# A hybrid decoder layer: the merge's gate and projection products made token-major, their sum turned for the output projection

## The chip, the core and the metric

The kernel runs on one core of one Trainium2 chip. The metric is the device time of one execution in microseconds. The engines of a core run their own instruction queues and wait for one another by semaphores: TensorE (PE; its weight loads are listed apart as PEld), VectorE (DVE), ScalarE (ACT), GpSimd (POOL), and SyncE (SP), which here only issues transfers from HBM.

## What is computed

One layer over 256 tokens of width 2048. Three branches (a gated linear recurrence "HGRN", causal pooling, a spatial gating unit) each give a 256 x 1024 result. The part that matters here merges them and projects the sum out:

```python
z = x @ w_in[l]
# the last 3 * 2048 columns of z are the gates, gr
gates = jax.nn.sigmoid(gr).reshape(B, S, 3, D)            # D = 2048
merged = (gates[:, :, 0] * (y_hg   @ w_hg_proj[l])        # each y: 256 x 1024
          + gates[:, :, 1] * (y_pool @ w_pool_proj[l])
          + gates[:, :, 2] * (y_sg   @ w_sg_proj[l]))
mix = merged @ w_out[l]
x = layer_norm(DN_ALPHA * x + mix, ln1_g[l], ln1_b[l])
```

A gated feed-forward network of width 5632 and a second layer norm follow.

## The kernel before

**Precision.** Every large product is made of float32 operands that are split in two float32r parts, high and low (`split`, L69: ACT copies the rounded high part, L70; DVE subtracts it from the source, L74). A product is high x high + high x low + low x high. The tile `X` holds the transposed input: for each of 16 blocks k of 128 features (a k-tile) 512 columns, the high parts of the 256 tokens and then their low parts. `y16` holds a branch's result in the same way, in 8 k-tiles.

**Weights.** `pieces` (L79) streams a weight matrix. SP fetches 1 MB pieces into one of two `raw` buffers; each piece is split in two stages of 128 x 1024 elements, into one of four `whi` buffers (ACT) and one of four `wlo` buffers (DVE). So ACT can be at most four stages ahead of PE, and a new piece is fetched when both stages of an older one are split.

**Two forms of a product.** `feat_major` (L114, its inner loop `fm_piece`, L104) makes 256 output features for all 256 tokens, features on the partitions. The weight is stationary, X moves: per k-tile and block of 128 features one matmul of 512 columns (L109, high weight against both parts of X) and one of 256 (L110, low weight against the high part). The low x high result stands in its own columns of the accumulator, so `fm_sum` (L180) adds the two halves afterwards: an ACT copy to `fm_low` and a DVE add. `tok_major` (L137) makes 512 output features with tokens on the partitions. X is stationary, the weight moves: per k-tile and block of 128 tokens three matmuls of 512 columns (L148, L149, L150) that add up in one accumulator. Accumulators are `mm` tiles, three of them; small results go to one of two `ax` tiles.

**The merge.** `merge` (L610) runs once for each branch, in the order pool, gating unit, HGRN. Each run has 8 steps of 256 features: a gate product of 16 k-tiles, `fm_sum` and a sigmoid on ACT; a projection product of 8 k-tiles, `fm_sum`, a multiplication by the gate, and (in the second and third run) an addition to `acc`. In the first two runs the recurrence of one half of the HGRN heads goes on beside it: `hgrn_steps` is a generator, `next(side)` after each product lets it emit its next part, which is DVE and ACT work and a few small PE products. Ahead of each of the first two runs `hgrn` makes six products for its half: four feature-major, a token-major one, two feature-major.

**After the merge.** `acc` is features x tokens, so it is split straight into `mT_t` (which takes the place of X) and used by `tok_major` with `w_out` (L711). Its four column blocks are added to x, and the layer norm follows. The pool `mix`, which holds `acc`, `y16` and the HGRN tiles, is given back before that.

**Order.** PE's order is that of the code. DVE, ACT and SP are ordered by the scheduler by priority; weight splits and the work under `hp()` go first.

Of the kernel before, what the change touches and what calls it, by code (L numbers as in the profile page):

```python
# [8 lines left out]
F32 = mybir.dt.float32  # L9
# [7 lines left out]
P = 128  # L17
S = 256
NT = S // P
# [22 lines left out]
def hybrid_layer(  # L42
# [91 lines left out]
                                         stop=kt == kt_n - 1)  # L134
        return ps

    def tok_major(w2, col, xT, kt_n, big=4, step=2, last=0, home=None, done=None, during={}, ends=(512,)):  # L137
        if last:
            ps = [mm_tile()[:, 0, :] for _ in range(NT)]
        else:  # L140
            both = mm_tile()
            ps = [both[:, t, :] for t in range(NT)]

        def go(kt, t, hi, lo, k, o=None, w=slice(0, 512), first=0):
            o = ps[t] if o is None else o
            xs = slice(t * P, (t + 1) * P)
            xl = slice(S + t * P, S + (t + 1) * P)
            nc.tensor.matmul(o[:, w], lhsT=xT(kt)[:, xs], rhs=hi[:, k, w], start=kt == first, stop=False)  # L148
            nc.tensor.matmul(o[:, w], lhsT=xT(kt)[:, xs], rhs=lo[:, k, w], start=False, stop=False)  # L149
            nc.tensor.matmul(o[:, w], lhsT=xT(kt)[:, xl], rhs=hi[:, k, w], start=False, stop=kt == kt_n - 1)  # L150

        kept = []
        for k0, n, hi, lo in pieces(w2, col, 512, kt_n, big, step, home=home):
            if k0 < kt_n - last:
                for k in range(n):
                    for t in range(NT):
                        go(k0 + k, t, hi, lo, k)
            else:
                kept.append((k0, n, hi, lo))
                for k in range(n):  # L160
                    go(k0 + k, 0, hi, lo, k)
        if last:
            done(0, ps[0], 0, 512)
        c0 = 0
        for c1 in ends if last else ():
            left = last
            o = mm_tile()[:, 0, :] if c0 else ps[1]
            for k0, n, hi, lo in kept:
                for k in range(n):
                    go(k0 + k, 1, hi, lo, k, o, slice(c0, c1), kept[0][0] if c0 else 0)  # L170
                    left -= 1
                    for f in during.get(left, ()):
                        f()
            done(1, o, c0, c1)
            c0 = c1
        return ps
# [27 lines left out]
    one_c, eps_c, mhalf_c, zero_c = (cc[:, i:i + 1] for i in range(4))  # L204

    def rstd_of(pool, st, want_nmr=True):
        mv = pool.tile([P, 4], F32, name="ln_mv", bufs=2)
        nc.vector.bn_aggr(out=mv[:, 0:2], in_=st)
        nc.vector.tensor_scalar(out=mv[:, 1:2], in0=mv[:, 1:2], scalar1=LN_EPS, scalar2=None, op0=ALU.add)
        nc.gpsimd.tensor_tensor(out=mv[:, 1:2], in0=mv[:, 1:2], in1=mhalf_c, op=ALU.pow)  # L210
        if want_nmr:
            nc.vector.tensor_scalar(out=mv[:, 2:3], in0=mv[:, 0:1], scalar1=-1.0, scalar2=None, op0=ALU.mult)
            nc.gpsimd.tensor_tensor(out=mv[:, 2:3], in0=mv[:, 2:3], in1=mv[:, 1:2], op=ALU.mult)  # L213
        return mv[:, 0:1], mv[:, 1:2], mv[:, 2:3]
# [24 lines left out]
    def fm_a():  # L239
        return mix.tile([P, 2, S], F32, name="fm_a", bufs=2)  # L240
# [364 lines left out]
            stt(o[:, hs], o[:, hs], normg[:, h0 + h:h0 + h + 1], og[:, hs], ALU.mult, ALU.mult)  # L605
        res.append(bc(o, S))

    acc = mix.tile([P, KD, S], F32, name="acc")

    def merge(first, gi, y, wp, side=()):  # L610
        side = iter(side)
        gcol = 7168 + D * gi
        for j in range(8):
            ps = feat_major(win, gcol + 256 * j, xT, KD)
            gt = fm_a()
            fm_sum(gt, ps, mix)
            with hp():
                act(gt, gt, AF.Sigmoid)
            next(side, None)
            ps = feat_major(wp, 256 * j, lambda k: y[:, k, :], KW)  # L620
            aj = acc[:, 2 * j:2 * j + 2, :]
            pr = fm_b()
            fm_sum(pr, ps, mix)
            with hp():
                if first:
                    mul(aj, pr, gt)
                else:
                    mul(pr, pr, gt)
                    add(aj, aj, pr)
            next(side, None)  # L630
        for _ in side:
            pass

    o_hg = []
    merge(True, 1, y_pool, w_pool_proj[0], hgrn_steps(0, *hgrn(0), o_hg))
# [1 line left out]
    split(y_hg[:, 0:4, 0:S], y_hg[:, 0:4, S:2 * S], o_hg[0])  # L637
    merge(False, 2, y_sg, w_sg_proj[0], hgrn_steps(1, *hgrn(1), o_hg))
    split(y_hg[:, 4:8, 0:S], y_hg[:, 4:8, S:2 * S], o_hg[1])
    merge(False, 0, y_hg, w_hg_proj[0])  # L640
    mT_t = x_tile()
    for j in range(8):
        split(mT_t[:, 2 * j:2 * j + 2, 0:S], mT_t[:, 2 * j:2 * j + 2, S:2 * S], acc[:, 2 * j:2 * j + 2, :])
    mix_cm.__exit__(None, None, None)

    def mT(k):
        return mT_t[:, k, :]

    ff_cm = tc.tile_pool(name="ff", bufs=1, reuse_waits="tile")
    ff = ff_cm.__enter__()  # L650
# [57 lines left out]

    for j in range(3):
        cs = slice(512 * j, 512 * (j + 1))  # L710
        ps = tok_major(wout, 512 * j, mT, KD)  # L711
        with hp():
            for t in range(NT):
                stt(x1[:, t, cs], x1[:, t, cs], ALPHA, ps[t], ALU.mult, ALU.add)
                nc.vector.bn_stats(out=st1[:, t, j, :], in_=x1[:, t, cs])
# [206 lines left out]
```

## Time and profile before

| what | us |
|---|---|
| median of 3 runs (1602.33, 1602.33, 1611.42) | 1602.33 |
| the profiled execution | 1603.08 |
| its span, first to last instruction | 1601.4 |
| PE busy | 1582.5 |
| DVE busy | 1030.9 |
| ACT busy | 868.3 |
| merge runs, by the span's clock | 245.6 to 392.2, 481.0 to 627.6, 627.6 to 763.0 |

The profile takes one execution apart. Each instruction has a line of the kernel, an engine, the tiles that it writes and reads, a start and a duration. Matmuls are pipelined: a matmul's own duration is longer than the distance to the next one's start, so for PE the distance between starts is what counts, and a stretch with known numbers of matmuls gives it. "PEclk" is the granted TensorE clock as a share of the full 2.4 GHz. In the tile names buffer numbers are left out: `t` is `t4`, `y` is `y16`.

### The profile page before, as it was taken

What the parts mean: (1) busy time and instruction counts of PE and PEld (TensorE: products, weight loads), DVE (VectorE), ACT (ScalarE), POOL (GpSimd) and SP (SyncE); (2) the same over time, 40 slices, a digit from 0 to 9 for tenths busy, and PEclk for the clock granted to TensorE, in tenths of its full rate; (3) what the DMA queues carried; (4) which work ended last, traced back from release to release, by engine and by line L of the source; (5) the groups of instructions that cost most, each with busy time, mean ns of one, the idle gap of its engine ahead of it and who ended that gap; (6) DMA issues with size and microseconds to landing.
All of it is one profiled execution on the core that took longest, in us unless ns stands there. A gap on an engine that the chain in (4) does not pass through costs nothing. (4 is left out here: it accounts for less than half of the span.)

```text
span 1601.4 us, 21561 instructions
## 1 busy us (share of the span) xinstructions
PE 1582.5 (99%) x8673; PEld 1369.0 (85%) x8673; DVE 1030.9 (64%) x1244; ACT 868.3 (54%) x1022; POOL 48.6 (3%) x116
## 2 busy tenths in 40 slices
PE   9999999999999999999998999999999999999997
PEld 7888888888888888888888888888888888888886
DVE  6666547876448866665657766676666766455446
ACT  5555558766458756544435555555555555433332
POOL 1100000000000000000004000000000000000001
PEclk9999999999999999999999999999999999999998
DMA  7656565554555556655763555555565556655553
GB/s 252 230 185 196 184 202 167 183 184 158 184 186 182 177 170 206 210 185 184 244 206 129 184 188 195 196 185 184 190 197 192 184 186 235 210 185 198 196 186 130
DMA packets 254084, 305.20 MB, mean 191 GB/s; under 512 B 5148, under 2 KB 211540, under 8 KB 253472
## 3 DMA queue, kind: packets, MB, share of 16 engines
q1 hardware_dynamic: 251776, 294.67, 56.1%
q0 software_dynamic: 2208, 9.16, 1.6%
q8 instruction: 68, 1.11, 0.3%
q14 instruction: 32, 0.26, 0.1%
HBM read 301.71 MB, written 2.10 MB: 190 GB/s over the span
## 5 line engine op out<-in xcount | busy, mean ns | idle before, releaser
L74 DVE TENSOR_TENSOR wlo<-raw,whi 128x1024 fp32r<-128x1024 f32 x541 | 659.9, 1222 | 502.4 <-ACT whi L70 500.8
L70 ACT ACTIVATE whi<-raw 128x1024 fp32r<-128x1024 f32 x543 | 571.5, 1056 | 647.6 <-PE mm L109 366.2
L109 PE MATMUL mm<-X,whi 128*128 128x512 f32 x1408 | 495.5, 397 | 0.5 <-DVE X L74 0.4
L109 PE MATMUL mm<-x1T,whi 128*128 128x512 f32 x1376 | 477.1, 394 | 0.0
L110 PE MATMUL mm<-X,wlo 128*128 128x256 f32 x1408 | 394.0, 280 | 0.0
L110 PE MATMUL mm<-x1T,wlo 128*128 128x256 f32 x1376 | 381.9, 278 | 0.0
L109 PEld LDWEIGHTS mm<-X,whi 128*128 128x128 f32 x1408 | 265.0, 188 | 62.7 <-PE mm L270 0.6
L109 PEld LDWEIGHTS mm<-x1T,whi 128*128 128x128 f32 x1376 | 258.8, 188 | 59.4
L110 PEld LDWEIGHTS mm<-X,wlo 128*128 128x128 f32 x1408 | 265.7, 189 | 0.2
L110 PEld LDWEIGHTS mm<-x1T,wlo 128*128 128x128 f32 x1376 | 258.2, 188 | 0.0
L109 PE MATMUL mm<-y,whi 128*128 128x512 f32 x384 | 137.2, 397 | 0.0
L148 PE MATMUL mm<-whi,aT 128*128 128x512 f32 (+1 forms) x352 | 135.5, 385 | 0.0
L150 PE MATMUL mm<-whi,aT 128*128 128x512 f32 (+1 forms) x352 | 135.4, 385 | 0.0
L149 PE MATMUL mm<-wlo,aT 128*128 128x512 f32 (+1 forms) x352 | 135.4, 385 | 0.0
L110 PE MATMUL mm<-y,wlo 128*128 128x256 f32 x384 | 108.4, 282 | 0.0
L148 PE MATMUL mm<-whi,X 128*128 128x512 f32 x228 | 88.9, 390 | 0.0
L150 PE MATMUL mm<-whi,X 128*128 128x512 f32 x228 | 88.9, 390 | 0.0
L149 PE MATMUL mm<-wlo,X 128*128 128x512 f32 x228 | 88.8, 390 | 0.0
L109 PEld LDWEIGHTS mm<-y,whi 128*128 128x128 f32 x384 | 72.4, 188 | 16.8
L150 PEld LDWEIGHTS mm<-whi,aT 128*128 128x128 f32 x352 | 66.2, 188 | 13.1
L149 PEld LDWEIGHTS mm<-wlo,aT 128*128 128x128 f32 x352 | 66.2, 188 | 13.1
L148 PEld LDWEIGHTS mm<-whi,aT 128*128 128x128 f32 x352 | 66.2, 188 | 12.9
(180 smaller groups left out, 1221.1 us busy)
## 6 DMA issues: line engine op xcount, KB each, us to landing
raw<-in_w_in_dram SPq DMA_DIRECT2D x102, 1024.0 KB, 5.0
raw<-in_w_up_dram SPq DMA_DIRECT2D x88, 1024.0 KB, 5.1
raw<-in_w_down_dram SPq DMA_DIRECT2D x44, 1024.0 KB, 5.0
raw<-in_w_out_dram SPq DMA_DIRECT2D x16, 1024.0 KB, 5.1
raw<-in_w_pool_proj_dram SPq DMA_DIRECT2D x8, 1024.0 KB, 5.3
raw<-in_w_sg_proj_dram SPq DMA_DIRECT2D x8, 1024.0 KB, 5.3
raw<-in_w_hg_proj_dram SPq DMA_DIRECT2D x8, 1024.0 KB, 5.3
x<-in_x_dram POOLq DMA_DIRECT2D x4, 512.0 KB, 9.1
```

Of the source, the lines that this page charges most:

```text
L70: nc.scalar.activation(out=o, in_=a, func=f, **kw)
L74: low.tensor_tensor(out=lo, in0=src, in1=hi.bitcast(F32), op=ALU.subtract)
L109: nc.tensor.matmul(ps[:, c, :], lhsT=hi[:, k, cs], rhs=xT(kt)[:, 0:512], start=kt == 0, stop=False)
L110: nc.tensor.matmul(ps[:, c, 0:256], lhsT=lo[:, k, cs], rhs=xT(kt)[:, 0:256], start=False, stop=kt == kt_n - 1)
L148: nc.tensor.matmul(o[:, w], lhsT=xT(kt)[:, xs], rhs=hi[:, k, w], start=kt == first, stop=False)
L149: nc.tensor.matmul(o[:, w], lhsT=xT(kt)[:, xs], rhs=lo[:, k, w], start=False, stop=False)
L150: nc.tensor.matmul(o[:, w], lhsT=xT(kt)[:, xl], rhs=hi[:, k, w], start=False, stop=kt == kt_n - 1)
```

## The change

The merge's gate and projection products are made by `tok_major` in blocks of 512 features, four blocks to a run instead of eight steps of 256. `acc` becomes tokens x features. The sigmoid reads the accumulator directly, the product with the gate too; `fm_sum` is not called in the merge. The generator's parts are now emitted after the gate product's k-tiles 4 and 10 (the new argument `mid` of `tok_major`), after the gate product, and after the projection product. The third run is written apart, as `last_merge`: first the four gate products, kept in a tile that takes the place of `y_sg`, then the four projection products. As `acc` now has tokens on the partitions, TensorE turns it: `turn(j)` transposes eight 128 x 128 blocks into two `ax` tiles and splits them into `mT_t`, in the middle of the next projection product, and for the last block in the middle of the first output product, which is now issued ahead of giving back `mix`. The tile `ln_mv` grows from 4 to 16 floats, by which tiles allocated behind it move by 64 bytes (in `mix`: `lv`, `masks`, `y16`, `fm_a`, `fm_b`, `sc`; later the kept output weights and all tiles of the feed-forward stage).

```diff
--- before.py
+++ after.py
@@ -134,7 +134,7 @@
                                          stop=kt == kt_n - 1)
         return ps
 
-    def tok_major(w2, col, xT, kt_n, big=4, step=2, last=0, home=None, done=None, during={}, ends=(512,)):
+    def tok_major(w2, col, xT, kt_n, big=4, step=2, last=0, home=None, done=None, during={}, ends=(512,), mid={}):
         if last:
             ps = [mm_tile()[:, 0, :] for _ in range(NT)]
         else:
@@ -155,6 +155,8 @@
                 for k in range(n):
                     for t in range(NT):
                         go(k0 + k, t, hi, lo, k)
+                    for f in mid.get(k0 + k, ()):
+                        f()
             else:
                 kept.append((k0, n, hi, lo))
                 for k in range(n):
@@ -204,7 +206,7 @@
     one_c, eps_c, mhalf_c, zero_c = (cc[:, i:i + 1] for i in range(4))
 
     def rstd_of(pool, st, want_nmr=True):
-        mv = pool.tile([P, 4], F32, name="ln_mv", bufs=2)
+        mv = pool.tile([P, 16], F32, name="ln_mv", bufs=2)
         nc.vector.bn_aggr(out=mv[:, 0:2], in_=st)
         nc.vector.tensor_scalar(out=mv[:, 1:2], in0=mv[:, 1:2], scalar1=LN_EPS, scalar2=None, op0=ALU.add)
         nc.gpsimd.tensor_tensor(out=mv[:, 1:2], in0=mv[:, 1:2], in1=mhalf_c, op=ALU.pow)
@@ -605,31 +607,66 @@
             stt(o[:, hs], o[:, hs], normg[:, h0 + h:h0 + h + 1], og[:, hs], ALU.mult, ALU.mult)
         res.append(bc(o, S))
 
-    acc = mix.tile([P, KD, S], F32, name="acc")
-
-    def merge(first, gi, y, wp, side=()):
+    acc = mix.tile([P, NT, D], F32, name="acc")
+
+    def columns(j):
+        return slice(512 * j, 512 * (j + 1))
+
+    def open_gate(gi, j, home, mid={}):
+        ps = tok_major(win, 7168 + D * gi + 512 * j, xT, KD, mid=mid)
+        with hp():
+            for t in range(NT):
+                act(home[t], ps[t], AF.Sigmoid)
+
+    def pass_gate(first, j, y, wp, home, mid={}):
+        ps = tok_major(wp, 512 * j, lambda k: y[:, k, :], KW, mid=mid)
+        with hp():
+            for t in range(NT):
+                at = acc[:, t, columns(j)]
+                if first:
+                    mul(at, ps[t], home[t])
+                else:
+                    mul(home[t], ps[t], home[t])
+                    add(at, at, home[t])
+
+    def gates():
+        return [fm_a().rearrange("p c s -> p (c s)") for _ in range(NT)]
+
+    def merge(first, gi, y, wp, side):
         side = iter(side)
-        gcol = 7168 + D * gi
-        for j in range(8):
-            ps = feat_major(win, gcol + 256 * j, xT, KD)
-            gt = fm_a()
-            fm_sum(gt, ps, mix)
-            with hp():
-                act(gt, gt, AF.Sigmoid)
+
+        def step():
             next(side, None)
-            ps = feat_major(wp, 256 * j, lambda k: y[:, k, :], KW)
-            aj = acc[:, 2 * j:2 * j + 2, :]
-            pr = fm_b()
-            fm_sum(pr, ps, mix)
-            with hp():
-                if first:
-                    mul(aj, pr, gt)
-                else:
-                    mul(pr, pr, gt)
-                    add(aj, aj, pr)
-            next(side, None)
+
+        for j in range(4):
+            home = gates()
+            open_gate(gi, j, home, {4: [step], 10: [step]})
+            step()
+            pass_gate(first, j, y, wp, home)
+            step()
         for _ in side:
             pass
+
+    def last_merge(gi, y, wp):
+        kept = mix.tile([P, 8, 512], F32, name="y16", bufs=2)
+        homes = [[kept[:, 2 * j + t, :] for t in range(NT)] for j in range(4)]
+        for j in range(4):
+            open_gate(gi, j, homes[j])
+        mT_t = x_tile()
+
+        def turn(j):
+            for t in range(NT):
+                with hp():
+                    tp = bc(ax_tile(), P)
+                    for i in range(4):
+                        k = 4 * j + i
+                        nc.tensor.transpose(tp[:, i, :], acc[:, t, k * P:(k + 1) * P], ident)
+                    to = mT_t[:, 4 * j:4 * j + 4, :]
+                    split(to[:, :, t * P:(t + 1) * P], to[:, :, S + t * P:S + (t + 1) * P], tp)
+
+        for j in range(4):
+            pass_gate(False, j, y, wp, homes[j], {KW - 3: [lambda j=j: turn(j - 1)]} if j else {})
+        return mT_t, {6: [lambda: turn(3)]}
 
     o_hg = []
     merge(True, 1, y_pool, w_pool_proj[0], hgrn_steps(0, *hgrn(0), o_hg))
@@ -637,14 +674,13 @@
     split(y_hg[:, 0:4, 0:S], y_hg[:, 0:4, S:2 * S], o_hg[0])
     merge(False, 2, y_sg, w_sg_proj[0], hgrn_steps(1, *hgrn(1), o_hg))
     split(y_hg[:, 4:8, 0:S], y_hg[:, 4:8, S:2 * S], o_hg[1])
-    merge(False, 0, y_hg, w_hg_proj[0])
-    mT_t = x_tile()
-    for j in range(8):
-        split(mT_t[:, 2 * j:2 * j + 2, 0:S], mT_t[:, 2 * j:2 * j + 2, S:2 * S], acc[:, 2 * j:2 * j + 2, :])
-    mix_cm.__exit__(None, None, None)
+    mT_t, turn_last = last_merge(0, y_hg, w_hg_proj[0])
 
     def mT(k):
         return mT_t[:, k, :]
+
+    first_out = tok_major(wout, 0, mT, KD, mid=turn_last)
+    mix_cm.__exit__(None, None, None)
 
     ff_cm = tc.tile_pool(name="ff", bufs=1, reuse_waits="tile")
     ff = ff_cm.__enter__()
@@ -708,7 +744,7 @@
 
     for j in range(3):
         cs = slice(512 * j, 512 * (j + 1))
-        ps = tok_major(wout, 512 * j, mT, KD)
+        ps = tok_major(wout, 512 * j, mT, KD) if j else first_out
         with hp():
             for t in range(NT):
                 stt(x1[:, t, cs], x1[:, t, cs], ALPHA, ps[t], ALU.mult, ALU.add)
```

On DVE, in the first run's beginning, before the change: the rows from the addition that prepares the recurrence's decay. `wlo` rows are weight stages, here those of the second gate product and the first of the second projection; `t4`, `seg` and `lv` rows are the recurrence.

```order
L61 TENSOR_TENSOR t4_2225<-t4_2225,t4_1456 128x1024
L74 TENSOR_TENSOR wlo_2402<-raw_2399,whi_2401 128x1024
L481 SCALAR_TENSOR_TENSOR t4_2241<-seg_78,t4_2225 128x256 x3
L74 TENSOR_TENSOR wlo_2422<-raw_2399,whi_2421 128x1024
L481 SCALAR_TENSOR_TENSOR t4_2241<-seg_78,t4_2225 128x256
L58 TENSOR_TENSOR t4_2225<-t4_2241,t4_2224 128x4x128 x2
L58 TENSOR_TENSOR lv_2446<-t4_2241 128x512
L74 TENSOR_TENSOR wlo_2458<-raw_2455,whi_2457 128x1024
L64 TENSOR_TENSOR t4_2224<-t4_2224,t4_1457 128x1024
L74 TENSOR_TENSOR wlo_2478<-raw_2455,whi_2477 128x1024
L61 TENSOR_TENSOR fm_a_2393<-mm_2308,fm_low_2394 128x512
L74 TENSOR_TENSOR t4_2251<-t4_2224,t4_2250 128x1024
```

The same place after the change, from the same addition on; `wlo_2315`, `wlo_2331` and `wlo_2349` are the first three of the four stages of the first projection product.

```order
L61 TENSOR_TENSOR t4_2184<-t4_2184,t4_1456 128x1024
L74 TENSOR_TENSOR wlo_2315<-raw_2312,whi_2314 128x1024
L483 SCALAR_TENSOR_TENSOR t4_2200<-seg_78,t4_2184 128x256 x4
L58 TENSOR_TENSOR t4_2184<-t4_2200,t4_2183 128x4x128 x2
L74 TENSOR_TENSOR wlo_2331<-raw_2312,whi_2330 128x1024
L58 TENSOR_TENSOR lv_2382<-t4_2200 128x512
L64 TENSOR_TENSOR t4_2183<-t4_2183,t4_1457 128x1024
L74 TENSOR_TENSOR wlo_2349<-raw_2346,whi_2348 128x1024
L64 TENSOR_TENSOR lv_2382<-lv_2382,t4_1457 128x512
L74 TENSOR_TENSOR t4_2210<-t4_2183,t4_2209 128x1024
L58 TENSOR_TENSOR lv_2386<-t4_2200,t4_2184 128x4x64 x2
L58 TENSOR_TENSOR lv_2447<-t4_2200 128x512
```

The same recurrence work moved up: one more pair of subtractions follows, and then the fourth stage, so that all of it stands among four weight stages, where before it was spread over about eight.

On PE, in the last projection products after the change: the transposes of the first block (two groups of four, into the two `ax` tiles) stand between the sixth and the seventh k-tile of the second projection product (`mm_5552`).

```order
L149 MATMUL mm_5552<-wlo_5590,y16_3182 128x512
L150 MATMUL mm_5552<-whi_5589,y16_3182 128x512
L663 MATMUL ax_5605<-id2_69,acc_1455 128x128 x4
L663 MATMUL ax_5612<-id2_69,acc_1455 128x128 x4
L148 MATMUL mm_5552<-whi_5619,y16_3182 128x512
L149 MATMUL mm_5552<-wlo_5620,y16_3182 128x512
```

Before the change the last projection product runs into the first output product with nothing between them.

```order
L109 MATMUL mm_6496<-y16_3438,whi_6519 128x512
L110 MATMUL mm_6496<-y16_3438,wlo_6520 128x256
L148 MATMUL mm_6580<-whi_6583,X_6545 128x512
L149 MATMUL mm_6580<-wlo_6584,X_6545 128x512
L150 MATMUL mm_6580<-whi_6583,X_6545 128x512
```

Four such groups of eight transposes are new on PE, and the pairs of 512 and 256 columns have given way to triples of 512.

## Rows read from the trace of the kernel before

**Rows 1.** The page, busy time of each engine, with share and instructions.

```profile
PE 1582.5 (99%) x8673; PEld 1369.0 (85%) x8673; DVE 1030.9 (64%) x1244; ACT 868.3 (54%) x1022; POOL 48.6 (3%) x116
```

**Rows 2.** Waits of PE: waiting line, releaser, total us, times, longest.

```profile
PE ax L700 <- issue: 1.9, 1, 1.9
...
PE mm L109 <- DVE X L74: 0.4, 1, 0.4
```

**Rows 3.** Waits of ACT, its two costliest: releaser, us in total, times, longest.

```profile
ACT whi L70 <- PE mm L109: 366.2, 283, 2.6
ACT whi L70 <- PE mm L150: 169.3, 107, 4.3
```

**Rows 4.** PE by stretches: window, length, busy (matmuls touching it), clock, DMA, GB/s.

```profile
627.60:763.00 135.40, 135.40 (x770) 1.00 0.63 204
763.00:831.00 68.00, 68.00 (x302) 1.00 0.64 224
245.60:392.20 146.60, 146.60 (x868) 1.00 0.55 176
481.00:627.60 146.60, 146.60 (x868) 1.00 0.54 173
263.00:274.10 11.10, 11.10 (x65) 1.00 0.55 178
644.40:655.70 11.30, 11.30 (x66) 1.00 0.72 224
392.20:436.60 44.40, 44.40 (x258) 1.00 0.57 187
458.40:481.00 22.60, 22.60 (x129) 1.00 0.54 170
```

**Rows 5.** PE's timeline at the layer norm's transposes: start, us, engine, line, operation.

```profile
848.02 0.66 PE L700 MATMUL ax<-id,x 128*128 128x128 f32 x4 [1.17 <-POOL x L695]
848.44 0.47 PE L148 MATMUL mm<-khi,X 128*128 128x512 f32 x1
...
849.67 0.40 PE L150 MATMUL mm<-khi,X 128*128 128x512 f32 x1
849.91 0.60 PE L700 MATMUL ax<-id,x 128*128 128x128 f32 x4
850.26 0.48 PE L148 MATMUL mm<-khi,X 128*128 128x512 f32 x1
```

**Rows 6.** PE's timeline at another group of eight transposes.

```profile
57.51 1.03 PE L361 MATMUL ax<-id,t 128*128 128x128 f32 x8
58.30 0.48 PE L148 MATMUL mm<-whi,X 128*128 128x512 f32 x1
```

**Rows 7.** The layer norm's transposes as instructions on the tile ax: duration ns min/median/max.

```profile
L700 PE MATMUL ax<-id,x x32: 272/273/329, 848.0 to 867.7; 128*128 128x128 f32 x32
```

**Rows 8.** ACT and DVE groups of the third run: count, busy us, mean ns, idle.

```profile
L70 ACT ACTIVATE whi<-raw 128x1024 fp32r<-128x1024 f32 x48 | 50.4, 1059 | 69.9 <-PE mm L109 53.3 <-DMA raw<-in_w_in_dram 7.9 <-DMA raw<-in_w_hg_proj_dram 7.7
L70 ACT ACTIVATE fm_low<-mm 128x512 f32<-128x512 f32 x16 | 9.3, 578 | 0.0
...
L74 DVE TENSOR_TENSOR wlo<-raw,whi 128x1024 fp32r<-128x1024 f32 x49 | 59.6, 1224 | 55.5 <-ACT whi L70 55.5
...
L61 DVE TENSOR_TENSOR fm_b<-mm,fm_low 128x512 f32<-128x512 f32 x8 | 5.5, 684 | 0.0
```

**Rows 9.** DVE's instructions on the tile t4 in one stretch: length, busy (count).

```profile
267.40:286.40 19.00, 10.74 (x16) 1.00 0.53 168
```

**Rows 10.** DMA issues of the merge's weights: count, KB each, median us to landing.

```profile
raw<-in_w_in_dram SPq DMA_DIRECT2D x102, 1024.0 KB, 5.0
raw<-in_w_pool_proj_dram SPq DMA_DIRECT2D x8, 1024.0 KB, 5.3
```

## The prediction

> **What bounds the kernel now.** I read the page's busy times first. PE is busy for 1582.5 of 1601.4 us, DVE and ACT for about two thirds and a half [rows 1]. A busy PE is not yet a bound, so the next view is the list of PE's waits. The longest in the whole span is 1.9 us, at the first layer norm, and the only one that falls on a product beside it is 0.4 us at the start [rows 2]. In the merge PE waits for nothing. The view from the other side agrees: ACT, which makes the high parts of the weights, stands 366.2 and 169.3 us waiting for PE to give back a weight buffer [rows 3]. So the weights are ahead, the engines that feed PE have room, and in the merge time is PE's own: number of matmuls by the distance from one to the next.
>
> That distance comes from stretches with known counts. The third run of the merge has 8 x (64 + 32) = 768 matmuls of the feature-major form in 135.4 us (the view counts 770, two only touch the stretch): 176.3 ns each, half of them 512 and half 256 columns wide [rows 4]. Right behind it 300 token-major matmuls of 512 columns, three full output products and two k-tiles, take 68.0 us: 226.7 ns each [rows 4]. The granted clock is 1.00, the 2.4 GHz level, in both. A k-tile for 512 features needs eight of the first kind, 1.410 us, or six of the second, 1.360 us. The columns are as many (3072). What differs is that each matmul costs a little beyond its columns, and there are two fewer.
>
> **The change part by part.** *Products.* The third run's 768 matmuls become 576: 576 x 0.2267 = 130.6 us for 135.4, a gain of 4.8. The first two runs have the same 768, with 98 or 100 small ones between. Some of their gate products run at 11.1 us where those of the third need 11.3 [rows 4], so I take 4.6 each. Together -14.0 (bound -14.4, if they equal the third).
>
> *Interruptions.* The small products of the recurrence stay, in eleven groups to a run, but now stand in token-major streams. Rows show what a group does there: after four transposes the six matmuls of a k-tile run from 848.44 to 849.91, 1.47 us where six at 226.7 need 1.36 [rows 5]. That is 0.11 us lost to each restart. The removed form's figures had their restarts in them, so I add 11 x 0.11 x 2 = +2.4. Bounds: 0, if a restart costs as in the old form, and +3.
>
> *Transposes.* Four groups of eight are new on PE. Eight like them take 0.79 us (57.51 to 58.30) [rows 6], four 0.42 or 0.35 [rows 5]. With a restart a group of eight is 0.9: +3.7 in all, between 3.1 without restarts and 3.8. Their own durations are 0.27 us [rows 7], but the next starts 0.1 us later. The Trainium skill, page "TensorE: Matmul & The Clock Gate", Part 4, gives about 275 ns for a transpose within a kernel; the duration in the trace agrees, the spacing doesn't, and by that figure per transpose 32 would cost an estimated 8.8 us and most of the gain would be gone.
>
> *State of the stream.* Feature-major products run at two rates: the 256 matmuls of the second half's first four products take 44.4 us (173.4 each), and the 128 that follow a token-major product 22.6 (176.6) [rows 4]. After the change those 256 follow a token-major product too: 256 x 3.2 ns = +0.8. Bounds 0 and 0.8.
>
> *ACT and DVE.* The calls of `fm_sum` go: 48 copies of 0.578 us and 48 additions of 0.684 [rows 8], 27.7 us of ACT and 32.8 of DVE. They had cover, PE never waited for them, so this gives nothing back. Sigmoids, gate multiplications, additions to `acc` and splits into `mT_t` keep number and size. The splits now read what PE turned. The last ones follow the seventh k-tile of the first output product and are needed by its k-tile 12, five k-tiles or 6.8 us later; four operations of 0.6 to 0.7 us fit. The turn of a block stands six k-tiles, 8.2 us, behind the end of the product that made it, and four DVE operations of 0.7 us need to be done by then. In `last_merge` the four gate products need `y_sg`'s tile, whose last reader is PE just before; the first write is a sigmoid 21.8 us later. The weights stay 1 MB a piece, in the same number.
>
> *The grown tile.* The 64-byte moves change no shape or count. I cost them at nothing; if the rate of the down projection, 1056 matmuls, moved by the 3.2 ns above, it would be 3.4 us.
>
> *The weights' lead.* This is where cover could end. With four buffers a stage can be split once PE has done the one four before it, so it is ready 3 x 2.72 us, less 1.06 and 1.22 for its two halves [rows 8], ahead: 5.9 us. At the start of the first two runs the recurrence's preparation stands on DVE among four weight stages, as the order shows: 16 instructions, 10.7 us [rows 9]. With four stages of 1.22 that is 15.6 us, in which PE does four stages and one small group, 11.3 us. The lead falls by 4.3 to about 1.6 us, at the projection's last stage. I take no stall, and up to one late landing of 5.3 us [rows 10] to a run as a bound.
>
> *Sum.* -14.0 + 2.4 + 3.7 + 0.8 = -7.1 us. The profiled execution has 1601.4 of span and 1603.08 in all, 0.05% over the median, so the span should fall to 1594.3 and the median from 1602.33 to **1595.2**.
>
> **The rivals.**
> *The weights run late (slower).* Place: the first projection product of the first two runs, where the lead is thin. If ACT's exponentials, which stand in one queue with the weight copies and wait for DVE's results, add more than 1.6 us to DVE's stretch, PE waits. A stage split late also gives its `raw` buffer back late, so that the next fetch, 5.3 us, shows. It decides from 3.6 us of stall to a run on, where the gain is gone. At one exposed landing to each run: 1595.2 + 10.6 = 1605.8. For it: the crowding just counted. Against it: about 536 us of ACT waiting for PE's buffers, so the lead recovers everywhere else [rows 3].
>
> *Nothing is gained by the form.* If a matmul's time went by its columns alone, 512 of them would be two thirds of a pair of the old form, 2/3 x 2 x 176.3 = 235 ns, six of these 1.410 us, and the products would cost what they did. Then the additions remain: 1602.33 + 2.4 + 3.7 + 0.8 = 1609.2. Against it stand the 300 matmuls at 226.7 with the same stationary X and the same moving weights [rows 4]. The Trainium skill, page "TensorE: Matmul & The Clock Gate", section Back-to-back issue gap, is near this rival: columns over 2.4 GHz and 2.5 ns. By that a k-tile would be an estimated 1.300 us in the old form and 1.295 in the new, 1.5 us over the 288 k-tiles, and the change a loss. The trace's spacing for 512 columns is 226.7 ns rather than 215.8, so here it is too small.
>
> *More is gained.* Restarts cost no more than in the old form, the stream keeps its faster rate, and the transposes cost 3.1: -14.4 + 3.1 = -11.3, which is 1591.0. Against it the 0.11 us of the restart row.
>
> **How the numbers follow.** About 1% (16 us) is what a measurement of this kernel can tell from no change. The forecast, a gain of 5 to 9 us, has 0.60; more gain 0.14; late weights 0.16; no gain by the form 0.05; the rest, an effect of the moved tiles or a stall in the transposes, 0.05. The range from 1590.5 to 1604 takes in the forecast, the greater gain and the milder half of the late weights, with some 0.83. A gain of over 1% would need 16 us, more than all the product gain: 0.03. A loss of over 1% needs waits in most of the blocks of all runs: 0.05. Within 1%: 0.92.
>
> **What the profile after would show.** Products: the stretch of the third run to the first output product has 576 matmuls of token-major form at about 227 ns between starts; 230 or more would break the largest term. Restarts: the k-tile behind a group of small products takes about 1.47 us. Transposes: 0.8 us between the start of the first of eight and the next product. Late weights: waits of PE on DVE's `wlo` near the first projection products, about 25 us into the first and second run; with none over half a microsecond that rival falls. ACT's table loads and DVE's busy time should fall with no trace of it in the span. I am wrong if PE's waits rise by over 3 us, or if feed-forward or down projection change their length.

## The result and the profile after

The changed kernel takes 1616.03 us (median of 20 executions) against 1602.67 for the kernel before: 1.0053 times as long [1.0036, 1.0069]. The forecast was 1595.2, between 1590.5 and 1604. So it lies within the 1% that can hardly be told from no change, but on the other side of it, and outside the range. Nineteen executions stand in two groups, 7 at 1606.7 to 1609.2 us and 12 at 1615.1 to 1619.6 (one more, of 2440.73 us at a granted clock of 0.60, is left aside). The two groups turn out to be part of the answer. The profiled execution, 1615.63 us with a span of 1613.9, is one of the upper group.

The page after, first the busy times. Against [rows 1] DVE and ACT are relieved by 28 and 39 us. The removed calls of `fm_sum` make 32.8 us of DVE's work and 27.7 of ACT's [rows 8], and ACT's table loads fell as well, from 46 to 34 (59.0 us to 43.6). PE is busy 13 us longer with 544 instructions fewer.

```profile
PE 1595.4 (99%) x8129; PEld 1349.1 (84%) x8129; DVE 1002.7 (62%) x1196; ACT 829.0 (51%) x962; POOL 47.9 (3%) x116
```

The span cut at PE's stages tells where the time went. Columns: window, length, then busy time and count of PE, PEld, DVE, ACT and POOL, granted clock, DMA share, GB/s. First before: merge, output products with the layer norm, up products of the feed-forward network, down projection (a tail of 28 us behind it is as long in both).

```profile
245.60:763.00 517.40, 517.40 (x2982) 453.20 (x2981) 345.13 (x410) 324.99 (x381) 4.03 (x6) 1.00 0.57 184
763.00:873.30 110.30, 106.09 (x546) 89.98 (x545) 73.66 (x83) 48.55 (x55) 17.60 (x14) 1.00 0.54 186
873.30:1350.40 477.10, 477.10 (x2755) 417.63 (x2754) 329.55 (x430) 271.42 (x345) 5.44 (x44) 1.00 0.59 193
1350.40:1573.40 223.00, 223.00 (x986) 184.83 (x985) 111.54 (x102) 89.76 (x87) 0.00 (x0) 1.00 0.59 201
```

The same four stages after.

```profile
245.30:758.00 512.70, 512.18 (x2431) 427.46 (x2430) 317.00 (x364) 286.41 (x322) 4.04 (x6) 1.00 0.57 190
758.00:870.20 112.20, 108.66 (x553) 91.91 (x552) 72.56 (x81) 47.62 (x52) 17.22 (x14) 0.98 0.48 161
870.20:1356.40 486.20, 486.20 (x2754) 421.69 (x2754) 330.38 (x430) 271.56 (x345) 5.45 (x44) 1.00 0.58 189
1356.40:1586.00 229.60, 229.60 (x986) 185.04 (x985) 111.83 (x102) 89.79 (x87) 0.00 (x0) 1.00 0.57 196
```

The merge gained 4.7 us. The two largest losses are in stages whose code and instructions did not change: +9.1 in the up products (2752 matmuls, 173.4 ns each before and 176.7 after) and +6.6 in the down projection (984 matmuls, 226.7 and 233.3). PE waits in neither, and the clock is 1.00 in both. Output products and layer norm lose 1.9, of which 0.9 is the last group of transposes that now stands there. The other 1.0 goes with the clock, 0.98 in that stage: behind PE's wait of 2.0 us at the layer norm it stands near 0.5, the 1.2 GHz level, and six matmuls of 512 columns start 0.43 us apart, where 0.23 is usual.

```profile
849.50:852.00 2.50, 2.50 (x9) 0.53 0.95 304
```

In the profile of before the clock stays at 1.00 behind the same wait (1.9 us [rows 2]). It fell there in all six profiles with the new merge and in three of the seven with the old one, so whether the change has a part in it is not shown.

PE's waits after (waiting line, releaser, us in total, times, longest) have one new entry, half a microsecond for a low weight part; the others are those of [rows 2] and the start.

```profile
PE ax L736 <- issue: 2.0, 1, 2.0
...
PE mm L149 <- DVE wlo L74: 0.5, 1, 0.5
```

And ACT waits for PE's weight buffers as long as before: 287.8 and 285.5 us for 366.2 and 169.3 [rows 3]. The weights are ahead, so the time is still PE's own.

```profile
ACT whi L70 <- PE mm L150: 287.8, 182, 3.0
ACT whi L70 <- PE mm L109: 285.5, 222, 1.8
```

Inside the merge the new form has two rates. PE by stretches: 238 gate matmuls of the third run, on X, and 84 projection matmuls behind them, on `y16`.

```profile
655.00:709.00 54.00, 54.00 (x240) 1.00 0.58 194
710.80:730.30 19.50, 19.50 (x86) 1.00 0.55 191
```

That is 226.9 ns for the first, as forecast, but 232 for the second (232.4 by the starts, 710.77 to 730.29 us). PE's timeline at a group of transposes in the projection (start, us, operation) shows the forecast 0.79 us [rows 6], then a restart: the second matmul behind it starts 0.31 us after the first.

```profile
730.29 1.03 PE L663 MATMUL ax<-id,acc 128*128 128x128 f32 x8
731.08 0.48 PE L148 MATMUL mm<-whi,y 128*128 128x512 f32 x1
731.39 0.39 PE L149 MATMUL mm<-wlo,y 128*128 128x512 f32 x1
```

So three things need a cause: the rate of token-major products on `y16` and in the down projection, the rate of the up products, and the new wait.

### The profile page after: what moved, and what is told of

Read it like the earlier page. It is cut to its first block, busy times and chain, and to the rows that moved or that the text cites. A ratio compares the mean times of both kernels' runs of the same rounds, so it can differ in the third digit from the quotient of the medians.

```text
span 1613.9 us, 20294 instructions
## 1 busy us (share of the span) xinstructions
PE 1595.4 (99%) x8129; PEld 1349.1 (84%) x8129; DVE 1002.7 (62%) x1196; ACT 829.0 (51%) x962; POOL 47.9 (3%) x116
## 5 line engine op out<-in xcount | busy, mean ns | idle before, releaser
L70 ACT ACTIVATE whi<-raw 128x1024 fp32r<-128x1024 f32 x543 | 571.3, 1056 | 689.7 <-PE mm L150 287.8
L109 PE MATMUL mm<-x1T,whi 128*128 128x512 f32 x1376 | 486.3, 399 | 0.0
L110 PE MATMUL mm<-x1T,wlo 128*128 128x256 f32 x1376 | 386.5, 281 | 0.0
L148 PE MATMUL mm<-whi,X 128*128 128x512 f32 x612 | 239.5, 391 | 0.0
L149 PE MATMUL mm<-wlo,X 128*128 128x512 f32 x612 | 238.3, 389 | 0.5 <-DVE wlo L74 0.5
L150 PE MATMUL mm<-whi,X 128*128 128x512 f32 x612 | 238.3, 389 | 0.0
L109 PE MATMUL mm<-X,whi 128*128 128x512 f32 x640 | 225.3, 397 | 0.5 <-DVE X L74 0.4
L110 PE MATMUL mm<-X,wlo 128*128 128x256 f32 x640 | 179.1, 280 | 0.0
L109 PEld LDWEIGHTS mm<-X,whi 128*128 128x128 f32 x640 | 120.1, 188 | 29.2 <-DVE X L74 0.6
L149 PEld LDWEIGHTS mm<-wlo,X 128*128 128x128 f32 x612 | 114.9, 188 | 24.2 <-DVE wlo L74 1.1
L150 PEld LDWEIGHTS mm<-whi,X 128*128 128x128 f32 x612 | 114.9, 188 | 24.0
L148 PEld LDWEIGHTS mm<-whi,X 128*128 128x128 f32 x612 | 114.9, 188 | 23.5
L110 PEld LDWEIGHTS mm<-X,wlo 128*128 128x128 f32 x640 | 120.7, 189 | 0.1
```

Of the source, the lines that this page charges most:

```text
L70: nc.scalar.activation(out=o, in_=a, func=f, **kw)
L109: nc.tensor.matmul(ps[:, c, :], lhsT=hi[:, k, cs], rhs=xT(kt)[:, 0:512], start=kt == 0, stop=False)
L110: nc.tensor.matmul(ps[:, c, 0:256], lhsT=lo[:, k, cs], rhs=xT(kt)[:, 0:256], start=False, stop=kt == kt_n - 1)
```

## The experiments

**The token-major rate.** `aT`, the tile that the down projection holds stationary, is one of those that the growth of `ln_mv` moved by 64 bytes. My theory was that the place of the tile sets the distance between matmuls. The rival: something else in the changed program, such as the merge's new order or the layer norm's different timing. Two runs part them: the change without the growth, and the growth without the change.

```diff
--- the changed kernel
+++ e1_after_mv4
-        mv = pool.tile([P, 16], F32, name="ln_mv", bufs=2)
+        mv = pool.tile([P, 4], F32, name="ln_mv", bufs=2)
```

> The changed kernel with ln_mv at 4 floats again, so that y16 and aT lie where they lay before the change. Theory A (the address of the stationary tile sets the distance of token-major matmuls): the down projection's 984 first matmuls go back from 233.3 to 226.7 ns, so 6.5 us come back: about 1600.3 us, or 1609.5 in an execution whose feed-forward products run at their slower rate (486 us instead of 477). Theory B (the rates are states that a stream falls into by what ran before it, addresses do nothing): the down projection stays at 233.3 and the time stays at 1606.8 or 1616.

```diff
--- the kernel before
+++ e2_before_mv16
-        mv = pool.tile([P, 4], F32, name="ln_mv", bufs=2)
+        mv = pool.tile([P, 16], F32, name="ln_mv", bufs=2)
```

> The kernel before with ln_mv at 16 floats, nothing else: y16 and aT move by 64 bytes. Theory A (address): the down projection goes from 226.7 to 233.3 ns a matmul, 1602.5 + 6.5 = 1609 us, and if the feed-forward stage's slower rate comes with the move as well, mostly 1618. Theory B (state, by what ran before): 1602.5, as the kernel before.

PE by stretches, the down projection without the growth:

```profile
1349.00:1572.00 223.00, 223.00 (x985) 1.00 0.58 201
```

and the kernel before with the growth alone, its up products and its down projection:

```profile
876.40:1353.50 477.10, 477.10 (x2755) 1.00 0.58 193
1353.50:1583.10 229.60, 229.60 (x987) 1.00 0.57 195
```

The 6.6 us follow the growth, in both directions. As medians, the first takes 1603.12 us (1.0010 [0.9988, 1.0031]), in two groups again, 7 of 12 executions at 1600.9 to 1603.7 and 5 at 1610.7 to 1612.7. Its lower group is 5 us below that of the changed kernel, not 6.6: with `y16` at its old place the first 84 projection matmuls take 19.6 us (233.4 ns), and late weights cost some 2 us in the last run's gate products.

```profile
712.90:732.50 19.60, 19.60 (x86) 1.00 0.55 191
```

The second takes 1615.1 (1.0077 [1.0050, 1.0104]), again in two groups (1611.6 to 1615.1 and 1621.3 to 1621.9). That is some 3 us more than the down projection explains. In its profile the layer norm's stage has 1.1 of them, by the lower clock told of above, and the merge 2.0: its feature-major products run at a slower rate more often, the first run for example in 147.1 us where [rows 4] have 146.6.

```profile
245.60:392.70 147.10, 147.10 (x867) 1.00 0.54 175
```

The up products kept their rate in this profile, so the growth is not what sets it.

In e3 `ln_mv` grows in the pool `mix` alone, and there far enough that `y16` stands as `X` does, 384 bytes behind a multiple of 512. `aT` stays where it was before.

```diff
--- the changed kernel
+++ e3_y_as_X
-        mv = pool.tile([P, 16], F32, name="ln_mv", bufs=2)
+        mv = pool.tile([P, 32 if pool is mix else 4], F32, name="ln_mv", bufs=2)
```

> The changed kernel with ln_mv at 32 floats in the mix pool and 4 in the ff pool: aT lies as before the change, y16 at the same offset within 512 bytes as X (384). Theory A: projection products run at 226.8 instead of 232 to 234 ns, down projection at 226.7: 1606.8 - 6.5 - 3.5 = 1596.8 us where the feed-forward products run at their faster rate. Theory B: 1606.8 or 1616 as the changed kernel.

PE by stretches: the first gate product and the other three of the last run, its first 84 projection matmuls, and the down projection.

```profile
621.30:710.30 89.00, 87.71 (x385) 1.00 0.58 203
710.30:729.40 19.10, 19.10 (x86) 1.00 0.55 199
1355.30:1578.40 223.10, 223.10 (x986) 1.00 0.59 201
```

The projection has come down to 227 ns and the down projection is back. The median, 1607.02 us (0.9998 [0.9977, 1.0020]), tells little: 5 executions at 1598.1 to 1602.7, 7 at 1606.8 to 1609.6. The gate products, whose 384 matmuls should take 87.1, still take 89.0.

The map: the 22 tiles of `aT` in groups of three, each 64 bytes further than the last, in the kernel before. One execution then has several rates, if it is the place, and one if it isn't.

```diff
--- the kernel before
+++ e4_map
-    aT_t = [up.tile([P, 2, 2 * S], F32R, name=f"aT{j}", bufs=1) for j in range(KF // 2)]
+    aT_t = []
+    for j in range(KF // 2):
+        raw = up.tile([P, 4 * S + (16 if j % 3 == 2 else 0)], F32R, name=f"aT{'abcdefgh'[j // 3]}{j}", bufs=1)
+        aT_t.append(raw[:, 0:4 * S].rearrange("p (k s) -> p k s", s=2 * S))
```

> The kernel before with the 22 aT tiles in eight groups, named aTa to aTh, each group 64 bytes further on within 512 than the one before: offsets 128, 192, 256, 320, 384, 448, 0, 64. Theory A: the distance of the down projection's matmuls changes from group to group, aTa 226.7 and aTb 233.3 ns, the others show which offsets are slow. Theory B: one distance over all groups, or changes that do not follow the groups in all four column blocks.

PE's timeline, the last matmul of each group of 36 in one column block: the steps between them are 8.18, 8.40, 8.36, 8.25 and 8.19 us.

```profile
1410.36 0.39 PE L150 MATMUL mm<-whi,aTh 128*128 128x512 f32 x1
...
1418.54 0.39 PE L150 MATMUL mm<-whi,aTa 128*128 128x512 f32 x1
...
1426.94 0.39 PE L150 MATMUL mm<-whi,aTb 128*128 128x512 f32 x1
...
1435.30 0.40 PE L150 MATMUL mm<-whi,aTc 128*128 128x512 f32 x1
...
1443.55 0.39 PE L150 MATMUL mm<-whi,aTd 128*128 128x512 f32 x1
...
1451.74 0.39 PE L150 MATMUL mm<-whi,aTe 128*128 128x512 f32 x1
```

Group a has 227.2 ns, b 233.3, c 232.4, d 229.1 (over all column blocks), and with e the pattern begins again and goes on through f, g and h: it repeats every 256 bytes. That leaves two readings, the place of the stationary tile by itself or its distance to the moving weight stages, which stand 384 bytes behind a multiple of 512 in all kernels so far. The next run moves the weight stages and `aT` by 64 bytes together; `X` stays, and so comes to another distance.

```diff
--- e4_map
+++ e8_map_w64
-    cc = const.tile([P, 4], F32, name="cc")
+    cc = const.tile([P, 20], F32, name="cc")
```

> The kernel before with the eight aT groups, and with a constant tile 64 bytes larger, so that the weight stages lie at 448 within 512 bytes instead of 384 and the groups at 192, 256, 320, 384, 448, 0, 64, 128. X stays at 384. Theory A1 (the stationary tile's own offset counts): groups at 384 and 128 (aTd, aTh) run at 227 ns, aTa at 233.3, and the output products with X at 226.8. Theory A2 (its distance from the moving weight's offset, within 256, counts): aTa and aTe run at 227, aTb at 233.3, aTc at 232.4, as before the shift, and the output products with X, now 64 bytes short of the weights, at 229 to 230.

PE's timeline, group ends as above, with steps of 8.39 (b), 8.37 (c), 8.25 us (d):

```profile
1434.78 0.39 PE L150 MATMUL mm<-whi,aTa 128*128 128x512 f32 x1
...
1443.17 0.39 PE L150 MATMUL mm<-whi,aTb 128*128 128x512 f32 x1
...
1451.54 0.40 PE L150 MATMUL mm<-whi,aTc 128*128 128x512 f32 x1
...
1459.79 0.39 PE L150 MATMUL mm<-whi,aTd 128*128 128x512 f32 x1
```

and the 300 token-major matmuls on `X`, which took 68.00 in [rows 4]:

```profile
768.60:837.30 68.70, 68.70 (x302) 1.00 0.64 223
```

Every group of `aT` stands 64 bytes further than in the map before and has kept its rate, so the place by itself falls. `X`, which has not moved, has gone from 226.7 to 229.0 ns at a distance of 192. What counts is the distance between the two operands, modulo 256 bytes. This execution took 1622.44 us, the one of the map 1606.23; 9 of the 16 us between them are up products at the slower rate (486.2 us), the others came up by the end of the merge.

The Trainium skill, page "TensorE: Matmul & The Clock Gate", section Back-to-back issue gap, lets the distance between isolated matmuls follow from the columns alone (by its formula an estimated 215.8 ns for 512) and gives about 131 ns for a stream of them. The Trainium skill, page "SBUF — State Buffer", section Who interferes with whom, calls PE's two reads, of moving operand and of weights, independent. The measured 226.7 to 233.3 ns fit neither figure, and neither page leads one to expect that they depend on the distance between the two operands; the measurement decides.

**The up products.** Two theories: the rate is a state that the stream of alternating 512 and 256 columns takes at its start and keeps; or something steady, such as addresses or DMA traffic, slows it. Against the second speak e1 and e2, where 477.1 occurs with and without the change. Nor did the operands move: not every tile of the feed-forward stage lies behind `ln_mv`, and `x1T`, which the up products move, stands like the weight stages at 384 behind a multiple of 512 in both kernels. A transpose ahead of each product makes the stream start anew 43 times; a pair of float32r matmuls of 512 columns puts something between without a change of type.

```diff
--- the kernel before
+++ e5_ff_turn
+                nc.tensor.transpose(ax_tile()[:, 0:P], ident, ident)
                 ps = feat_major(wup, half * DFF + 256 * j, x1T, KD, ready=() if j else chain(up_early, up_next))
```

> The kernel before with one transpose of the identity into an ax tile (never read) ahead of each of the 43 feed-forward up products. It asks what sets the two rates of the feature-major stream (173.4 and 176.7 ns a matmul, 11.09 and 11.31 us a product). Theory S (a state that a stream falls into where it starts, by a chance of timing, and keeps): each of the 43 products draws anew, some run at 11.1 and some at 11.3 us beside the 0.1 to 0.2 us of the transpose. Theory P (set by the program's tiles or by the execution as a whole): all 43 alike.

```diff
--- the kernel before
+++ e6_ff_fixed
+                tpx = ax_tile()
+                for i in range(2):
+                    nc.tensor.matmul(tpx, lhsT=fixed[:, 1, :], rhs=x1T(i), start=i == 0, stop=i == 1)
                 ps = feat_major(wup, half * DFF + 256 * j, x1T, KD, ready=() if j else chain(up_early, up_next))
```

> As the run with a transpose ahead of each feed-forward up product, but with two float32r matmuls of 512 columns (stationary identity, moving input) instead. Theory S: the products draw anew, and if the state depends on what runs just before, the shares differ from those behind a transpose: in the merge before, the gate products behind such a pair ran at 173.4 ns. Theory P: all 43 at one rate.

With transposes, PE by stretches: the first product of 64 matmuls and the second.

```profile
871.70:883.00 11.30, 11.30 (x67) 1.00 0.62 200
883.10:894.30 11.20, 11.20 (x68) 1.00 0.64 207
```

By the starts of their first matmuls (871.67, 883.08, 894.30 us) the first takes 11.41 us, and those behind it 11.21 each: the quicker 11.09 and 0.12 for the transpose with its restart. The first one, although it stands behind a transpose too, still has the slower rate. The one execution took 1606.45. With pairs of matmuls (1628.81 us) the first four products of the loop are:

```profile
875.10:886.20 11.10, 11.10 (x66) 1.00 0.63 205
886.70:897.80 11.10, 11.10 (x66) 1.00 0.61 199
898.20:909.50 11.30, 11.30 (x65) 1.00 0.55 179
910.00:921.30 11.30, 11.30 (x66) 1.00 0.51 166
```

and so on, two and two, through all 43. Both rates occur in one execution, on the same tiles at the same addresses. So the rate is a state of the stream. A small operation ahead can change it, and without one it lasts. What the pair changes in it, and why with a period of four, I can't say.

The merge of the kernel before has this state too. Its third run is the same code on the same addresses in e4, e5, e6 and e10 (which comes below). It takes 135.7 us in the last two, near the 135.4 of [rows 4], but 133.7 in e5 and 133.5 in e4:

```profile
627.60:761.10 133.50, 133.50 (x771) 1.00 0.63 207
```

So the 176.3 ns that the prediction starts from are the slower rate; at the quicker one the same matmuls take 173.8.

**The late weights.** After the change the load of `gb` (2 MB, for the layer norm) is issued earlier. GpSimd's timeline, before:

```profile
624.94 2.94 POOL L656 DMA_DIRECT2D x<-in_x_dram  x4 [517.06 <-PE mm L109]
760.68 0.57 POOL L662 DMA_DIRECT2D gb<-in_ln_g_dram  x1 [132.80 <-DVE fm_a L61]
```

and after:

```profile
605.37 2.94 POOL L692 DMA_DIRECT2D x<-in_x_dram  x4 [498.13 <-PE ax L507]
614.75 0.57 POOL L698 DMA_DIRECT2D gb<-in_ln_g_dram  x1 [6.44 <-DVE t L67]
```

Before, `gb` waited for the last additions of `fm_sum` in the merge (`fm_a`), whose helper tile `fm_low` lies where `gb` goes; these are gone, and both loads fall together. Between 612 and 620 us the DMA engines are full (share 1.00, 384 GB/s; before 0.39 and 131). ACT's waits for weights between 600 and 660 us, after:

```profile
ACT whi L70 <- DMA raw<-in_w_in_dram: 24.2, 7, 5.5
```

Before they were 9.3 us there. PE's timeline shows what comes through, one gap of 0.91 us where 0.23 is usual:

```profile
631.07 0.39 PE L148 MATMUL mm<-whi,X 128*128 128x512 f32 x1
631.98 0.50 PE L149 MATMUL mm<-wlo,X 128*128 128x512 f32 x1 [0.52 <-DVE wlo L74]
```

The run e7 holds `gb` back until the last merge's `mT_t` has its first values, with `y16` placed as `X`.

```diff
--- e3_y_as_X
+++ e7_gb_later
+    for c in range(2):
+        nc.gpsimd.tensor_tensor(out=gb1[:, c, 0:1], in0=mT_t[:, 0, 0:1].bitcast(F32), in1=zero_c, op=ALU.mult)
```

> The changed kernel with y16 at X's offset and aT as before the change (as the run named e3_y_as_X), and the load of the layer norm's two constant rows (2 MB, gb1) held back until the first turned block is there, by two one-element GpSimd operations. Theory: the stall of 0.7 to 2 us in the last run's first gate product comes from 4 MB of POOL loads beside the weight pieces, the 2 MB of gb1 having moved up by 146 us; held back, ACT's waits for w_in pieces between 600 and 660 us fall from 24 to about 10 us, the stall goes, and the time is 1596.2 us with fast feed-forward products, 1605.4 with slow. If the stall were DVE's crowding, it stays and the time is 1598.2 or 1607.4.

PE by stretches: the four gate products of the last run, the first projection matmuls, the up products.

```profile
622.60:709.60 87.00, 87.00 (x385) 1.00 0.61 199
709.60:728.70 19.10, 19.10 (x86) 1.00 0.56 194
867.40:1353.60 486.20, 486.20 (x2754) 1.00 0.58 189
```

The load is now issued at 730.46 us and the gate products have lost their stall (87.0 us for 384 matmuls, 89.0 in e3). ACT still waits 16.5 us for weights there, more than the 10 expected. The median is 1600.42 (0.9966 [0.9940, 0.9992]): 6 executions at 1595.1 to 1596.8, 6 at 1604.0 to 1606.5. What is left between the groups is, by the profiles, the up products' state: the after, e3 and e7 profiles are of the upper group and have 486.2 us there, those of e1 and e2 are of the lower group and have 477.

**Three kernels with the up products at one rate.** If transposes at its start bring the stream to the quicker rate, the kernels can be compared without the up products' state. I put one ahead of the first three products of the loop only, in the kernel before, in the changed one and in e7.

```diff
--- the kernel before, the changed kernel, e7_gb_later
+++ e10_before_turn, e11_after_turn, e9_best_turn
+                if j < 2:
+                    nc.tensor.transpose(ax_tile()[:, 0:P], ident, ident)
                 ps = feat_major(wup, half * DFF + 256 * j, x1T, KD, ready=() if j else chain(up_early, up_next))
```

> The kernel before with one transpose of the identity (an ax tile that nobody reads) ahead of each of the first three feed-forward up products of the loop. In the run with 43 of them the first product behind a transpose was slow, 11.38 us, and all later ones fast. Theory S (where the stream starts sets its rate, and after at most three such restarts it is the fast one): no execution at 1611 to 1614 us any more, all at 1602.5 + 0.4. Theory P (the execution as a whole sets it): 1 or 2 in 10 still at 1612.

> The changed kernel with the same three transposes. Theory S: its executions at 1615 to 1619 us go, all lie at 1606.8 + 0.4, and against the kernel before with the same transposes the change costs 4.4 us (6.5 in the down projection, 3.5 in the products with y, against about 5 gained in the merge). Theory P: more than half still at 1616.

> The changed kernel with y16 at X's offset, aT as before the change, the layer norm's constant rows loaded later, and the three transposes. Theory S: all executions at 1595.5 + 0.4 us, 7 us under the kernel before. Theory P: half of them at 1605.

PE by stretches, the 41 products behind the third transpose, 2624 matmuls, in e10:

```profile
896.10:1351.00 454.90, 454.90 (x2627) 1.00 0.59 192
```

In e11 it is 454.9 us, in e9 454.8. All three have 173.4 ns, and none of their 35 executions stands in an upper group. The plain kernels had 22 of 89 there (before) and 12 of 19 (after). Medians: before 1603.91 (1602.59 to 1605.39), after 1607.67 (1606.73 to 1609.80), e9 1596.79 (1595.24 to 1597.60). Against the plain kernel before they stand at 0.9992 [0.9974, 1.0011], 1.0011 [0.9990, 1.0031] and 0.9946 [0.9926, 0.9965]. So with the up products at one rate the change as it was made costs 3.8 us, and e9 gains 7.1. That leaves one state open, the one in the third merge run of the kernel before, which is slow in e10's profile (135.7 us) and is worth 2 us; e9 has no feature-major products there. e9 is the best version. Its stages, merge to down projection, with PE's column alone, stand beside those of the first two tables:

```profile
246.20:754.70 508.50, 508.50 (x2431) 1.00 0.58 192
754.70:866.90 112.20, 108.78 (x554) 0.98 0.48 162
866.90:1344.50 477.60, 477.60 (x2758) 1.00 0.59 193
1344.50:1567.60 223.10, 223.10 (x987) 1.00 0.58 201
```

## Why the prediction was wrong

The sum of the change's own terms came out nearly right for the execution that it was read from, and left out three costs. By the profiles' spans, after is 12.5 us longer than before: the forecast -7.1, then +6.6 and about +3.3 from operand distances, +0.7 from a stall, and +9.1 from the up products' state, together +12.6. With the three taken away (e9 against e10, the up products at one rate in both) the medians differ by 7.1 us. That these numbers agree so well is partly luck: in e9's profile the merge gained 8.9, where its part of the forecast was 8.0, and the stage behind it lost a microsecond to the clock that no term had. And up to 2 of the 7.1 hang on the slower rate of the third run before.

*Products*: right in kind. Token-major gate products take 226.7 ns a matmul. The step that failed is taking that figure, read on `X`, for the projection products on `y16` too: 576 matmuls at about 5.7 ns more are the 3.3 us. I had said that 230 or more would break the largest term; on `y16` it did. The other side of the term, 135.4 us for the third run, was one execution's rate: against the 133.5 of e4 the same 130.6 gain 2.9 and not 4.8, and I had given that figure no bound.

*Interruptions and transposes*: right. A group of eight took 0.79 us and a restart about 0.1.

*The grown tile*: failed. "I cost them at nothing", and the alternative beside it, 3.2 ns a matmul and 3.4 us, was half of what came, 6.6 ns and 6.6 us. The profile of before had shown that rates differ between tiles of the same form, and I took no bound from the chance that a moved tile changes rate.

*State of the stream*: the effect was named and sized (3.2 ns a matmul) and it came in the 256 matmuls where I put it (44.4 us to 45.2). The step failed by its reach. The same form has 2752 matmuls in the up products, where the same 3.2 ns are 9 us, and I took what the profiled execution showed there for a constant. The times of before already had one execution at 1611.42.

*ACT and DVE*: right, 39 and 28 us of relief gave nothing.

*The weights' lead*: the place was wrong. The first projection products, with 1.6 us of lead by my count, had no stall. The stall came in the last run's first gate product, from a transfer that the change released early. I had looked for transfers only in what the diff touches, and no line of it names `gb`.

*The rivals.* "The weights run late" had the sign and 1605.8 us, near the lower group of after, but not the cause. "Nothing is gained by the form" is refuted by e9, "more is gained" as well: e9 takes 1596.79, and the restarts do cost. The sentence that held is the last: I am wrong if feed-forward or down projection change their length.

Open: why the changed program starts its up products in the slower state in 12 of 19 executions and the kernel before in 22 of 89. e1, e3 and e7, which share its merge, have 5, 7 and 6 of 12, but e2, which doesn't, has 3 of 7. With so few executions neither the new merge nor the moved tiles can be singled out, and what at the stream's start decides is not shown, here or in the third merge run.

## What to carry to other kernels

A rate read on one pair of tiles holds for that pair: before carrying it over, or growing a small tile that others stand behind, compare the distances between stationary and moving operands. Where the executions of one kernel stand in two groups, find the stage that differs before costing a change by one profile, and fix that state in both kernels when comparing. When work is removed, look for transfers that its tiles held back.

## What the runs showed of the hardware

The spacing of float32r matmuls with 512 moving columns and a stationary tile of 128 depends on the distance of the two operands' addresses modulo 256 bytes: 226.7 to 227.2 ns at 0, 233.3 at 64, 232.4 at 128, 229.1 at 192 (stationary less moving), at a granted clock of 1.00. It was the same with both operands shifted by 64 bytes, and three stationary tiles show it: `aT`, `X` (229.0 at 192) and `y16` (233.4 at 64, 232.4 at 128). What in the chip does this is not shown.

A stream of alternating 512 and 256 columns with a new stationary weight for each has two rates, 173.4 and 176.7 ns a matmul, and kept the one that it had for hundreds of microseconds. With a transpose ahead of each of the first three products, at 0.12 us each, it was at the quicker one, by the times, in all 35 executions; in the four profiles with transposes the first product behind one was still slow, and all later ones quick. A pair of 512-column matmuls turned it over every second time.
